# A second raw chunk in the startup of a hybrid decoder step: 256-column chunks for four column tiles, and what is rescaled later

## The chip, the cores and the metric

The kernel runs on one core of one Trainium2 chip. The metric is the device time of one execution in microseconds (us), as a median over runs. Engines are named as in the profile: PE (TensorE, matrix products; PEld its weight loads), DVE (VectorE), ACT (ScalarE), POOL (GpSimd), SP (SyncE, which issues most DMAs).

## The reference

One layer of a decoder trunk for 1024 prompt positions and 64 sample positions (8 sequences of 8), each a row of 1024 values. Cut to what matters:

```python
h = rmsnorm(x, g_norm)
proj = h @ w_in                       # 1024 x 3200, split into nine column groups
bg_a, cg_a, v_a, z_a, a_b, g_b, z_b, q_x, z_x = parts
conv_a = causal_dwconv(ctx_a, cg_a * v_a, w_conv_a, b_conv_a)       # 3 taps
out_a = bg_a * conv_a * silu(z_a)
u_b = a_b * sigmoid(g_b)
conv_b = causal_dwconv(ctx_b, u_b, w_conv_b, b_conv_b)              # 31 taps
out_b = silu(layernorm(conv_b)) * silu(z_b)
out_x = cross_attn(q_x, mk, mv) * silu(z_x)                         # 256 memory rows
y = rmsnorm(x + concat(out_a, out_b, out_x) @ w_out, g_final)
```

The new convolution states and the memory's keys and values are outputs too. All is float32.

## The kernel before, in words

**Products.** A float32 factor is split into a part `hi`, rounded to the form that PE takes at full rate, and the rest `lo`. Each product is three passes over the eight 128-row slabs of the 1024 channels: hi by hi, weights' lo by hi, weights' hi by activations' lo (`pass_`, `pass_k`). The transposed activations are `hh[k]` and `hl[k]` (k = 0 to 7), 1088 columns (positions) each; `w_in`'s columns are 25 tiles of 128 in the list `order`: a0, a1, a2, g0 (these four neighbour each other in `w_in` and share one load per slab, `hw_load`, `hw_hi`, `hw_lo`), then cg0, v0, bg0, g1, g2, q0, q1 and so on. A tile's positions are worked in chunks: the first `NHEAD` tiles use the list `HEAD`, all others `REST`. `proj(n, c)` is one tile and chunk: 24 products, then an eviction `evac` from PSUM.

**Normalising.** x is loaded as nine tiles of rows (`xt[0]` to `xt[8]`), transposed on PE (`x_tr`, four PSUM banks `SD` in turn), multiplied by g_norm and split (`x_ev_hi` on ACT, `x_ev_lo` on DVE). The row factor 1/rms is found by a `Norm` object: a square per row tile on ACT (`square`), a short chain (a root on ACT, five small DVE operations, `chain`, `factor`), and a scaling of each row tile (`scale` on DVE, `scale_act` on ACT). For chunk 0 the products start from raw, unscaled activations; the factor, as a row of 256 columns `rrow` on all partitions, is multiplied in when the bank is evicted (`take`, on DVE, where `rawc` is true; else a copy on ACT). Later `rescale(k)` brings `hh[k]` and `hl[k]` of that chunk to their scaled values for the tiles that come after: two DVE operations, an ACT copy, a DVE subtraction.

**Order.** `startup` is written out by hand, and its instructions keep the written order on each engine (`manual_schedule`). What comes after it is ordered by a planner with costs of its own, which may also place a ready later instruction between those of the startup. Side work is a list `steps`; `pass_` runs one of them after slab 3 and one after slab 7 (`None` is an empty place). Engines run their queues strictly in order. SBUF has 45 large buffers (`big`), PSUM four banks `MM` for products and four `SD` for the rest.

**The startup.** WARM products of the identity, the transposes of tiles 0 and 1, then the loop over slabs, in which `p(k, j)` is slab k, pass j, for four tiles of chunk 0; cg0's chunk 0 in a fifth bank (`pr4`); chunk 1 of all five with n1 (row tiles 2 to 4) scaled ahead; n2 (row tiles 5 to 8) scaled beside it; the transposes of chunk 2 as side steps of chunk 1's third pass. Then chunk 2 of the five tiles with the rescaling and the transposes of the parameters (`params_T`) as side work, and from tile 5 on three chunks per tile.

**Taps.** When g0's last chunk is evicted, `queue_taps` queues 31 operations of 1024 columns on DVE for each of three channel groups (the long convolution); `run_taps(taps_per(n))` issues some of them after each `proj`.

Of the kernel before, what the change touches and what calls it, by code (L numbers as in the profile page):

```python
# [12 lines left out]
ALU = mybir.AluOpType  # L13
# [14 lines left out]
L0, L1, L2 = 1, 3, 2  # L28
T1, T2 = 2, 2
TAPPRI = 100  # L30
WARM = 5

HEAD = [(0, 256), (256, 384), (640, 448)]
REST = [(0, 384), (384, 384), (768, 320)]
NHEAD = 5


NROW = 4
RAW = HEAD[0][1]


@with_exitstack
def hybrid_trunk_kernel(
# [62 lines left out]
    def dv(ns):  # L106
        dve_t[0] += ns
# [7 lines left out]
                taps.popleft()()  # L115

    def taps_per(n):
        return 3 if 5 <= n < 9 else T1 if n < 11 else T2

    def side():  # L120
        if steps:
# [42 lines left out]
    xt = [None] * 9  # L164
    xrows = [128] * 8 + [64]
    xcols = [i * 128 for i in range(9)]
    groups = [[0, 1], [2, 3, 4], [5, 6, 7, 8]]

    def x_src(i):
        return x_prompt[0, i * 128:(i + 1) * 128, :] if i < 8 else x_sample.rearrange("b t d -> (b t) d")  # L170
# [1 line left out]
    def x_load(i):  # L172
        xt[i] = xt[i] or B("x", cols=D)
        if xrows[i] < 128:
            G.memset(xt[i][xrows[i]:], 0.0)
        nc.sync.dma_start(xt[i][:xrows[i]], x_src(i))
# [42 lines left out]
    def rescale(k):  # L219
        a, b = hh[k][:, :RAW], hl[k][:, :RAW]  # L220
        t = B("t", cols=RAW)
        V.tensor_tensor(t, a.bitcast(F32), b.bitcast(F32), ALU.add)
        V.tensor_tensor(t, t, rrow[0], ALU.mult)
        S.copy(a, t)
        V.tensor_sub(b, t, a.bitcast(F32))
        dv(1000)

    def gm_T():
        ps = SD()
# [48 lines left out]
    def hw_load(k, q=nc.sync):  # L278
        if k % 2 == 0:
            hrw[k // 2] = B("wr", cols=D)  # L280
        c0 = order[0][2] * 128
        q.dma_start(hrw[k // 2][:, hsl(k)], w_in[0, k * 128:(k + 1) * 128, c0:c0 + 512])
# [9 lines left out]
        dv(602)  # L292

    def w_block(n, k, lo):
        if n < NROW:
            o = (k % 2) * 512 + n * 128
            return (hwl if lo else hwh)[k // 2][:, o:o + 128]
        return (wlo if lo else whi)[n][:, k * 128:(k + 1) * 128]
# [102 lines left out]

    rawc, rrow = [False], [None]

    def take(dst, ps, n):
        if rawc[0]:
            V.tensor_tensor(dst, ps[:, :n], rrow[0][:, :n], ALU.mult)
            dv(n / 0.96 + 70)
        else:
            S.copy(dst, ps[:, :n])
# [4 lines left out]
    def ev_a(c, ps, j):  # L414
        off, n, p, s = pieces(c)
        if c[0] == 0:
            u_p[j] = B("u")
            G.memset(u_p[j][:, 0:30], 0.0)
        take(u_p[j][:, 30 + off:30 + off + p], ps, p)
        if s:  # L420
            S.copy(us_new(j), tb(ps[:, p:n]))

    def ev_g(c, ps, j):
        off, n, p, s = pieces(c)
        if c[0] == 0:
            sig[j] = B("sig")
        if j == 0:
            take(sig[j][:, off:off + n], ps, n)
            if s:
                S.activation(sig[0], sig[0], AF.Sigmoid)  # L430
                V.tensor_tensor(u_p[0][:, 30:30 + SEQ], u_p[0][:, 30:30 + SEQ], sig[0][:, :SEQ], ALU.mult)
                dv(1140)
        else:
            S.activation(sig[j][:, off:off + n], ps[:, :n], AF.Sigmoid)  # L434
            u = u_p[j][:, 30 + off:30 + off + p]
            V.tensor_tensor(u, u, sig[j][:, off:off + p], ALU.mult)
            dv(p / 0.96 + 70)
        if s:
            V.tensor_tensor(us_new(j), us_new(j), tb(sig[j][:, SEQ:NT]), ALU.mult)
            V.tensor_copy(u_s[j][:, 304:334], u_p[j][:, SEQ:SEQ + 30])  # L440
            dv(250)
            queue_taps(j)
# [16 lines left out]
    def ev_cg(c, ps, j):  # L459
        off, n, _, _ = pieces(c)  # L460
        if c[0] == 0:
            cgt[0] = B("cg")
        take(cgt[0][:, off:off + n], ps, n)

    def ev_v(c, ps, j):
        off, n, p, s = pieces(c)
# [56 lines left out]
    def evac(n, c, ps):  # L523
        kind, j, _ = order[n]
        c = chunks(n)[c]
        rawc[0] = n < NHEAD and c[0] == 0
        if kind == "zA":
            ev_z(c, ps, j, tA[j])
        elif kind == "zB":
            ev_z(c, ps, 3 + j, accB[j])  # L530
        elif kind == "zX":
            ev_z(c, ps, 6 + j, aO[j])
        else:
            {"g": ev_g, "a": ev_a, "q": ev_q, "cg": ev_cg, "v": ev_v, "bg": ev_bg}[kind](c, ps, j)
# [461 lines left out]
    def startup():  # L996
# [8 lines left out]
        hw_load(2)  # L1005
        for i in (0, 1):
            x_half(i, 1, nc.sync)
        hw_load(3)
        x_load(2)
        hw_load(4)  # L1010
        hw_load(5)
        x_load(3)
        hw_load(6)
        hw_load(7)
        x_load(4)
        w_load(4)
        for i in range(5, 8):
            x_load(i)
        for k in range(KT):
            hh[k] = B("hh", F32R)  # L1020
# [4 lines left out]
        T.transpose(wps[:, 256:264], graw, ident[:8, :8])  # L1025
        V.tensor_copy(gT[:, 0:8], wps[:, 256:264])
        xt[8] = B("x", cols=D)
        norm = [Norm([xt[i] for i in g], [xrows[i] for i in g]) for g in groups]
        n0, n1, n2 = norm
        banks = [SD() for _ in range(4)]  # L1030

        def x0_tr(k, i):
# [2 lines left out]
        for i in (0, 1):  # L1035
            for k in range(4):
                x0_tr(k, i)
        acc = [MM() for _ in range(NROW)]

        def p(k, j):  # L1040
            for n in range(NROW):
                pass_k(n, 0, acc[n], j, k)

        def hi(k):
# [25 lines left out]
        mem_load()  # L1070
        load_params()
        nc.sync.dma_start(graw, g_mem[0].rearrange("(k p) -> k p", p=128))
        w_load(5)
        n0.square(0)
        hw_hi(3, S.copy)
        banks += [SD() for _ in range(4)]
# [7 lines left out]
        hw_lo(3)  # L1084
        for k in range(4, 8):
            lo(k)
        for k in range(3, KT):
            if k > 3:
                hw_hi(k, S.copy)
                hw_lo(k)  # L1090
            p(k, 0)
            p(k - 1, 1)
            p(k - 1, 2)
            if k == 5:
                n0.square(1)
                n0.chain()
                n0.factor()
                fb = B("fb", cols=RAW)
                for i in (0, 1):
                    V.tensor_scalar(  # L1100
                        fb[:, i * 128:i * 128 + 128], ident, 0.0, n0.f[:, i:i + 1], ALU.mult, ALU.add
                    )
            if k == 6:
                rps = SD()
                for i in (0, 1):
                    tr(rps[:, i * 128:i * 128 + 128], fb[:, i * 128:i * 128 + 128], 128)
                n1.square(0)
                rrow[0] = B("rrow", cols=RAW)
                S.copy(rrow[0], rps[:, :RAW])
        for n in range(NROW):  # L1110
            for j in (1, 2):
                pass_k(n, 0, acc[n], j, KT - 1)
        w_hi(4, G.tensor_copy)
        n1.square_v(1)
        n1.square(2)
        n1.chain()
        n1.factor()
        n1.scale_act(1)
        n1.scale(0)
        n1.scale(2)  # L1120
        w_lo(4)
        pr4 = SD()
        for n in range(NROW):
            evac(n, 0, acc[n])
        for j, (lo_, h) in enumerate(((False, hh), (False, hl), (True, hh))):
            for k in range(KT):
                mm(
                    pr4[:, :RAW], w_block(4, k, lo_), h[k][:, :RAW],
                    j == 0 and k == 0, j == 2 and k == KT - 1, RAW / 2.4,
                )  # L1130
        evac(4, 0, pr4)
        t1 = [x_tr(1, k) for k in range(3)]
        pr = [MM() for _ in range(NROW)]
        for k in range(KT):
            x_ev(1, k, t1[k])
            for n in range(NROW):
                pass_k(n, 1, pr[n], 0, k)
            if k + 3 < KT:
                t1.append(x_tr(1, k + 3))
        for i in range(4):  # L1140
            n2.square(i)
        n2.chain()
        n2.scale(0)
        n2.scale(1, G)
        n2.scale(2)
        n2.scale(3)
        for n in range(NROW):
            pass_(n, 1, pr[n], 1)
        mem_norm()
        for k in range(KT):  # L1150
            steps.append(mk(x_T, 2, k))
        for n in range(NROW):
            pass_(n, 1, pr[n], 2)
            evac(n, 1, pr[n])
        pr4 = MM()
        for j in range(3):
            pass_(4, 1, pr4, j)
        evac(4, 1, pr4)
        flush_steps()


    if True:
        with tc.manual_schedule():
            startup()
        for n in range(0, NCT):
            if n < NHEAD:
                if n == 0:
                    for k in range(KT):
                        steps += [mk(rescale, k)]
                    for h in range(2):  # L1170
                        steps.append(mk(w_split, NHEAD, h))
                    for j in range(3):
                        steps += [mk(params_T, j), None]
                    steps.append(gm_T)
                if n == 2:
                    w_load(NHEAD + 1)
            else:
                w_load(n + 2)
            kind, j, _ = order[n]
            if n == NHEAD:  # L1180
                for q in range(2):
# [68 lines left out]
            if n == 23:  # L1250
                for k in (0, 1):
                    steps += [None, mk(wo_split, worder[k], 0), None, mk(wo_split, worder[k], 1)]
                wo_load(worder[2])
            for c in range(3) if n >= NHEAD else (2,):
                proj(n, c)
                if c < 2:
                    w_split(n + 1, c)
# [57 lines left out]
```

## Time and profile before

| | |
|---|---|
| median of 3 runs | 478.25 us (477.37 to 479.23) |
| profiled execution, its own time | 477.41 us |
| its span | 475.3 us, 7295 instructions |
| busy: PE, DVE, ACT, POOL | 462.9, 325.5, 223.6, 8.2 us |
| chain that ended last | PE 67%, DVE 23%, ACT 5%, issue 3%, DMA 2% of the span |
| moved by DMA | 40.42 MB, mean 85 GB/s |

A row of a timeline gives the start, the duration (of a group: from its first start to its last end; products overlap, so the distance to the next group's start says what a group costs), the engine, the line, what was written from what, and in brackets how long the engine had been idle before and what released it. A row of waits gives the total, the count and the longest. Times are from the span's start.

### The profile page before, as it was taken

The numbers are of one execution on the slowest core, as the hardware profiler recorded it, in microseconds if no ns is written. First come the engines' busy times: TensorE is split into PE (matmuls) and PEld (weight loads), VectorE is DVE, ScalarE is ACT, GpSimd is POOL, SyncE is SP. The second block draws the span as 40 slices with busy tenths as digits, with TensorE's granted clock in tenths as the row PEclk, the third lists the DMA queues.
The fourth block names the chain that finished last, engine by engine and source line by source line (L and its number), as shares of the span: only waits on it lengthen the run. The fifth ranks groups of instructions, "written<-read, shape, count | busy, mean of one in ns | idle before, by whom it ended". The sixth has DMA issues, their size and how long they took to land.

```text
span 475.3 us, 7295 instructions
## 1 busy us (share of the span) xinstructions
PE 462.9 (97%) x2827; PEld 431.1 (91%) x2827; DVE 325.5 (68%) x576; ACT 223.6 (47%) x581; POOL 8.2 (2%) x24
## 2 busy tenths in 40 slices
PE   8999999999999999999999999999999999999994
PEld 7889989999999998999999999899999988888884
DVE  3768824999999999998589498733563547333334
ACT  5657513803427338546692464657863524211111
POOL 3101000000000000000000000000000000000000
PEclk9999999999999999999999999999999999999998
DMA  8940412210027300111020531022401643311111
GB/s 297 361 137 0 137 41 90 88 46 1 1 83 217 101 0 1 44 46 46 0 71 20 171 96 38 9 60 90 150 28 45 187 190 112 133 46 44 44 62 71
DMA packets 36446, 40.42 MB, mean 85 GB/s; under 512 B 1743, under 2 KB 30325, under 8 KB 36405
## 3 DMA queue, kind: packets, MB, share of 16 engines
q1 hardware_dynamic: 36109, 39.44, 25.8%
q10 hardware_dynamic: 304, 0.53, 0.4%
q8 instruction: 22, 0.36, 0.3%
q14 instruction: 11, 0.09, 0.1%
HBM read 34.81 MB, written 5.42 MB: 85 GB/s over the span
## 4 chain that ended last, share of the span: by engine, by line
PE 67%; DVE 23%; ACT 5%; issue 3%; DMA 2%; ACTq 0%; DVEq 0%; SPq 0%
PE mm L96 58%; DVE accB L60 11%; PE sd L103 5%; PE sd L96 3%; DVE wl L60 2%; DVE tA L60 2%; DVE Q L60 1%; DVE red L60 1%; DVE mx L60 1%; ACT sd L882 1%; DVE x L60 1%; ACT junk L188 1%; DMA wr<-in_w_in_dram 1%; DVE wml L60 1%; DMA graw<-in_g_norm_dram 1%
## 5 line engine op out<-in xcount | busy, mean ns | idle before, releaser
L96 PE MATMUL mm<-hh,wh 128*128 128x384 f32 (+3 forms) x592 | 117.1, 334 | 1.6 <-ACT wh L288 1.0
L96 PE MATMUL mm<-hl,wh 128*128 128x384 f32 (+3 forms) x592 | 116.8, 332 | 0.0
L60 DVE SCALAR_TENSOR_TENSOR accB<-u,prm,accB 128x1024 f32<-128x1024 f32 x90 | 115.2, 1281 | 1.2
L96 PE MATMUL mm<-hh,wl 128*128 128x384 f32 (+3 forms) x592 | 113.9, 330 | 0.0
L96 PEld LDWEIGHTS mm<-hh,wh 128*128 128x128 f32 x592 | 99.1, 190 | 5.2 <-ACT wh L288 1.5
L96 PEld LDWEIGHTS mm<-hl,wh 128*128 128x128 f32 x592 | 98.3, 188 | 2.0 <-issue 1.3
L96 PEld LDWEIGHTS mm<-hh,wl 128*128 128x128 f32 x592 | 99.0, 188 | 1.3 <-issue 0.3
L96 PE MATMUL mm<-woh,ml 128*128 128x512 f32 (+1 forms) x136 | 51.2, 377 | 0.0
L96 PE MATMUL mm<-wol,mh 128*128 128x512 f32 (+1 forms) x136 | 51.2, 377 | 0.0
L96 PE MATMUL mm<-woh,mh 128*128 128x512 f32 (+1 forms) x136 | 51.2, 377 | 0.0
L60 DVE TENSOR_TENSOR xres<-mm,xres 128x512 f32<-128x512 f32 (+2 forms) x19 | 12.4, 662 | 39.4 <-PE mm L96 39.2
L60 DVE TENSOR_TENSOR wl<-wr,wh 128x512 fp32r<-128x512 f32 x50 | 33.3, 686 | 5.1 <-ACT wh L288 2.7
L945 ACT ACTIVATE sd<-xres 128x512 f32<-128x512 f32 (+1 forms) x16 | 9.6, 600 | 57.6 <-DVE xres L60 57.6
L96 PEld LDWEIGHTS mm<-woh,mh 128*128 128x128 f32 x136 | 25.6, 188 | 4.7
L96 PEld LDWEIGHTS mm<-wol,mh 128*128 128x128 f32 x136 | 25.6, 188 | 4.7
L96 PEld LDWEIGHTS mm<-woh,ml 128*128 128x128 f32 x136 | 25.6, 188 | 4.6
L363 ACT ACTIVATE prod<-us,prm 128x64 f32<-128x64 f32 x93 | 24.0, 343 | 0.9 <-DVE wl L60 0.8
L713 ACT ACTIVATE P<-sd,nb 128x256 f32<-128x256 f32 x32 | 14.8, 474 | 18.9 <-DVE nb L60 18.8
L311 ACT CAST wh<-wr 128x512 fp32r<-128x512 f32 x40 | 23.3, 625 | 0.0
L511 ACT ACTIVATE sz<-mm 128x384 f32<-128x384 f32 (+1 forms) x24 | 11.3, 472 | 20.2 <-PE mm L96 20.2
L250 ACT ACTIVATE hh<-sd,gT 128x256 fp32r<-128x256 f32 (+2 forms) x24 | 12.8, 564 | 10.7 <-PE sd L103 10.4
L434 ACT ACTIVATE sig<-mm 128x384 f32<-128x384 f32 (+1 forms) x6 | 2.8, 473 | 31.4 <-PE mm L96 31.4
(206 smaller groups left out, 526.2 us busy)
## 6 DMA issues: line engine op xcount, KB each, us to landing
wr<-in_w_in_dram SPq DMA_DIRECT2D x21, 512.0 KB
wor<-in_w_out_dram SPq DMA_DIRECT2D x8, 512.0 KB
xres<-in_x_prompt_dram SPq DMA_DIRECT2D x8, 512.0 KB
out_dram<-xres SPq DMA_DIRECT2D x7, 512.0 KB
x<-in_x_prompt_dram SPq DMA_DIRECT2D x6, 512.0 KB
cache<-in_cache_mem_k_dram SPq DMA_DIRECT2D x8, 256.0 KB
cache<-in_cache_mem_v_dram SPq DMA_DIRECT2D x8, 256.0 KB
wr<-in_w_in_dram SPq DMA_DIRECT2D x7, 256.0 KB
```

Source lines behind the costliest of these rows:

```text
L60: r = f(*a, **k)
L96: T.matmul(out, lhsT, rhs, start=start, stop=stop)
L103: T.transpose(out, in_, ident[:n, :n])
L188: S.activation(junk[:r], self.ts[i][:r], AF.Square, accum_out=self.ss[:r, i:i + 1])
L250: S.activation(hh[k][:, off:off + n], ps[:, :n], AF.Copy, scale=gT[:, k:k + 1])
L311: S.copy(dst_hi[:, a:b], src[:, a:b])
L363: S.activation(p3[:, k, :], src, AF.Copy, scale=w[:, k0 + k:k0 + k + 1])
L434: S.activation(sig[j][:, off:off + n], ps[:, :n], AF.Sigmoid)
L511: S.activation(sz[0][:, off:off + n], ps[:, :n], AF.Silu)
L713: S.activation(P_[i][:, h * 256:h * 256 + 256], bank[h // 2][:, (h % 2) * 256:(h % 2) * 256 + 256], AF.Exp, bias=nb[:, h:h + 1], scale=SCA ...
L882: S.activation(junk[:, :384], t, AF.Square, bias=lst["nmu"][:, i:i + 1], accum_out=lst["sq"][:, i:i + 1])
L945: S.activation(junk[:rows], xr[:rows, cs], AF.Square, accum_out=ss[:rows, f:f + 1])
```

## The change

Four tiles instead of five are worked in `HEAD` chunks, and there are four such chunks of 256, 256, 256 and 320 columns instead of three of 256, 384 and 448. Chunks 0 and 1 of these tiles both start from raw activations (RAW = 512); `rrow` holds two scale rows of 256 and, beside each, the diagonal that is transposed into it (`r_bc`, `r_tr`, `r_cp`). `rescale` works on 512 columns. n1 is now row tiles 2 and 3 (only a factor, no scaling), n2 tiles 4 and 5, n3 tiles 6 to 8. cg0 becomes an ordinary tile with `REST` chunks; its weights are loaded behind the parameters. The hi and lo parts of slab 7 come ahead of the copy of the first scale row. x tile 2 is loaded behind slab 5 and tile 3 behind slab 7. There are nine warm-up products instead of five. In the last chunk the order of the tiles is a0, g0, a1, a2, and the taps per `proj` are 3 below tile 4, then 2. The memory's norm moves from the startup to a side step.

```diff
-WARM = 5
-HEAD = [(0, 256), (256, 384), (640, 448)]
+WARM = 9
+HEAD = [(0, 256), (256, 256), (512, 256), (768, 320)]
-NHEAD = 5
-NROW = 4
-RAW = HEAD[0][1]
+NHEAD = 4
+RAW = 512
-        return 3 if 5 <= n < 9 else T1 if n < 11 else T2
+        return 3 if n < NHEAD else T1 if n < 11 else T2
-    groups = [[0, 1], [2, 3, 4], [5, 6, 7, 8]]
+    groups = [[0, 1], [2, 3], [4, 5], [6, 7, 8]]
...
-        V.tensor_tensor(t, t, rrow[0], ALU.mult)
+        V.tensor_tensor(t, t, rrow[0][:, RAW:], ALU.mult)
...
-        rawc[0] = n < NHEAD and c[0] == 0
+        rawc[0] = n < NHEAD and c[0] < RAW
...
+        def r_bc(norm, off):
+            norm.chain()
+            norm.factor()
+            for i in (0, 1):
+                o = off + i * 128
+                V.tensor_scalar(rrow[0][:, o:o + 128], ident, 0.0, norm.f[:, i:i + 1], ALU.mult, ALU.add)
+        def r_tr(off):
+            ps = SD()
+            for i in (0, 1):
+                o = off + i * 128
+                tr(ps[:, i * 128:i * 128 + 128], rrow[0][:, o:o + 128], 128)
+            return ps
+        def r_cp(off, ps):
+            S.copy(rrow[0][:, RAW + off:RAW + off + 256], ps[:, :256])
...
             if k == 6:
-                rps = SD()
-                for i in (0, 1):
-                    tr(rps[:, i * 128:i * 128 + 128], fb[:, i * 128:i * 128 + 128], 128)
-                n1.square(0)
-                rrow[0] = B("rrow", cols=RAW)
-                S.copy(rrow[0], rps[:, :RAW])
+                rps = r_tr(0)
+                t1 += [x_tr(1, 0), x_tr(1, 1)]
+        r_cp(0, rps)
+        x_ev_hi(1, 0, t1[0])
+        x_ev_hi(1, 1, t1[1])
+        for n in range(NHEAD):
             for j in (1, 2):
                 pass_k(n, 0, acc[n], j, KT - 1)
-        (cg0's weight split, n1's squares, chain and three scalings, cg0's 24 products of chunk 0)
             evac(n, 0, acc[n])
+        t1 += [x_tr(1, 2), x_tr(1, 3)]
+        acc = [MM() for _ in range(NHEAD)]
         for k in range(KT):
+            if k > 1:
+                x_ev_hi(1, k, t1[k])
+            x_ev_lo(1, k, t1[k])
+            for n in range(NHEAD):
+                pass_k(n, 1, acc[n], 0, k)
+            if k + 4 < KT:
+                t1.append(x_tr(1, k + 4))
+        n1.square(0)
+        n1.square(1)
+        r_bc(n1, 256)
+        n2.square(0)
+        n2.square(1)
+        n2.chain()
+        n2.factor()
+        n2.scale_act(0)
+        n2.scale(1)
+        for n in range(NHEAD):
+            pass_(n, 1, acc[n], 1)
+        rps = r_tr(256)
+        r_cp(256, rps)
+        steps.extend([None, None])
         for k in range(KT):
             steps.append(mk(x_T, 2, k))
+        for i in range(3):
+            n3.square(i)
+        for n in range(NHEAD):
+            pass_(n, 1, acc[n], 2)
+            evac(n, 1, acc[n])
         flush_steps()
+        n3.chain()
+        n3.scale(0)
+        n3.scale(1)
+        n3.scale(2)
...
+        for k in range(KT):
+            steps.append(mk(x_T, 3, k))
+        for k in range(KT):
+            steps += [mk(rescale, k), None]
+        for n in range(NHEAD):
+            proj(n, 2)
+        w_load(NHEAD + 1)
+        for h in range(2):
+            steps.append(mk(w_split, NHEAD, h))
+        steps.append(mem_norm)
+        for j in range(3):
+            steps += [mk(params_T, j), None]
+        steps.append(gm_T)
+        for n in (0, 3, 1, 2):
+            proj(n, 3)
+        flush_steps()
```

More of the change, by code (lines that the diff above doesn't have):

```diff
@@ L222, in rescale @@
         V.tensor_tensor(t, a.bitcast(F32), b.bitcast(F32), ALU.add)
-        V.tensor_tensor(t, t, rrow[0], ALU.mult)
+        V.tensor_tensor(t, t, rrow[0][:, RAW:], ALU.mult)
         S.copy(a, t)
         V.tensor_sub(b, t, a.bitcast(F32))
-        dv(1000)
+        dv(1900)
     def gm_T():
@@ L294, in w_block @@
     def w_block(n, k, lo):
-        if n < NROW:
+        if n < NHEAD:
             o = (k % 2) * 512 + n * 128
@@ L402, in hybrid_trunk_kernel, with take @@
     rawc, rrow = [False], [None]
-    def take(dst, ps, n):
+    def take(dst, ps, off, n):
         if rawc[0]:
-            V.tensor_tensor(dst, ps[:, :n], rrow[0][:, :n], ALU.mult)
+            V.tensor_tensor(dst, ps[:, :n], rrow[0][:, RAW + off:RAW + off + n], ALU.mult)
             dv(n / 0.96 + 70)
@@ L418, in ev_a @@
             G.memset(u_p[j][:, 0:30], 0.0)
-        take(u_p[j][:, 30 + off:30 + off + p], ps, p)
+        take(u_p[j][:, 30 + off:30 + off + p], ps, off, p)
         if s:
@@ L427, in ev_g @@
         if j == 0:
-            take(sig[j][:, off:off + n], ps, n)
+            take(sig[j][:, off:off + n], ps, off, n)
             if s:
@@ L462, in ev_cg @@
             cgt[0] = B("cg")
-        take(cgt[0][:, off:off + n], ps, n)
+        take(cgt[0][:, off:off + n], ps, off, n)
     def ev_v(c, ps, j):
@@ L1007, in startup @@
             x_half(i, 1, nc.sync)
-        hw_load(3)
+        for k in (3, 4, 5):
+            hw_load(k)
         x_load(2)
[L1010 to L1017, printed above, removed]
+        for k in (6, 7):
+            hw_load(k)
+        for i in range(3, 8):
             x_load(i)
@@ L1027, in startup @@
         xt[8] = B("x", cols=D)
-        norm = [Norm([xt[i] for i in g], [xrows[i] for i in g]) for g in groups]
-        n0, n1, n2 = norm
+        n0, n1, n2, n3 = (Norm([xt[i] for i in g], [xrows[i] for i in g]) for g in groups)
+        rrow[0] = B("rrow", cols=2 * RAW)
+        def r_bc(norm, off):
[4 more added lines that the diff above has]
+                V.tensor_scalar(rrow[0][:, o:o + 128], ident, 0.0, norm.f[:, i:i + 1], ALU.mult, ALU.add)
+            dv(500)
+        def r_tr(off):
[6 more added lines that the diff above has]
+            S.copy(rrow[0][:, RAW + off:RAW + off + 256], ps[:, :256])
         banks = [SD() for _ in range(4)]
@@ L1037, in startup @@
                 x0_tr(k, i)
-        acc = [MM() for _ in range(NROW)]
+        acc = [MM() for _ in range(NHEAD)]
         def p(k, j):
-            for n in range(NROW):
+            for n in range(NHEAD):
                 pass_k(n, 0, acc[n], j, k)
@@ L1072, in startup @@
         nc.sync.dma_start(graw, g_mem[0].rearrange("(k p) -> k p", p=128))
-        w_load(5)
+        w_load(NHEAD)
         n0.square(0)
@@ L1086, in startup @@
             lo(k)
+        t1 = []
         for k in range(3, KT):
@@ L1095, in startup @@
                 n0.square(1)
-                n0.chain()
-                n0.factor()
-                fb = B("fb", cols=RAW)
-                for i in (0, 1):
-                    V.tensor_scalar(
-                        fb[:, i * 128:i * 128 + 128], ident, 0.0, n0.f[:, i:i + 1], ALU.mult, ALU.add
-                    )
-            if k == 6:
-                rps = SD()
-                for i in (0, 1):
-                    tr(rps[:, i * 128:i * 128 + 128], fb[:, i * 128:i * 128 + 128], 128)
-                n1.square(0)
-                rrow[0] = B("rrow", cols=RAW)
-                S.copy(rrow[0], rps[:, :RAW])
@@ L1110, in startup @@
-        for n in range(NROW):
+                r_bc(n0, 0)
+            if k == 6:
+                rps = r_tr(0)
[4 more added lines that the diff above has]
+        for n in range(NHEAD):
             for j in (1, 2):
                 pass_k(n, 0, acc[n], j, KT - 1)
[L1113 to L1123, printed above, removed]
-            evac(n, 0, acc[n])
[L1125 to L1132, printed above, removed]
@@ L1133, in startup @@
-        pr = [MM() for _ in range(NROW)]
-        for k in range(KT):
[L1135 to L1141, printed above, removed]
-        n2.chain()
[L1143 to L1149, printed above, removed]
+            evac(n, 0, acc[n])
@@ new lines, in startup @@
+        t1 += [x_tr(1, 2), x_tr(1, 3)]
+        acc = [MM() for _ in range(NHEAD)]
+        for k in range(KT):
+            if k > 1:
[10 more added lines that the diff above has]
+        n2.square(1)
+        n2.chain()
+        n2.factor()
@@ L1150, in startup @@
+        n2.scale_act(0)
[5 more added lines that the diff above has]
+        steps.extend([None, None])
         for k in range(KT):
             steps.append(mk(x_T, 2, k))
[L1152 to L1158, printed above, removed]
+        for i in range(3):
+            n3.square(i)
@@ L1164, in hybrid_trunk_kernel @@
             startup()
[L1165 to L1178, printed above, removed]
+        for k in range(KT):
+            steps.append(mk(x_T, 3, k))
+        for k in range(KT):
+            steps += [mk(rescale, k), None]
+        for n in range(NHEAD):
+            proj(n, 2)
[9 more added lines that the diff above has]
+        flush_steps()
+        for n in range(NHEAD, NCT):
+            w_load(n + 2)
             kind, j, _ = order[n]
@@ L1253, in hybrid_trunk_kernel @@
                 wo_load(worder[2])
-            for c in range(3) if n >= NHEAD else (2,):
+            for c in range(3):
                 proj(n, c)
```

## The prediction

> **What bounds the kernel now.** I read first the page's shares by engine, then the waits of TensorE, then the windows by stage, then the timelines of the first 60 us, where all of the change lies. The share and the waits:
>
> ```profile
> PE 462.9 (97%) x2827; PEld 431.1 (91%) x2827; DVE 325.5 (68%) x576; ACT 223.6 (47%) x581; POOL 8.2 (2%) x24
> ```
>
> ```profile
> PE mm L1024 <- POOL ss L183: 1.4, 1, 1.4
> PE sd L96 <- ACT PT L733: 1.1, 2, 0.6
> PE mm L96 <- ACT wh L288: 1.0, 1, 1.0
> PE mm L1025 <- DMA graw<-in_g_norm_dram: 0.8, 1, 0.8
> PE sd L96 <- DVE wl L60: 0.7, 1, 0.7
> PE mm L96 <- ACT wh L311: 0.6, 1, 0.6
> ACT L713 <- DVE nb L60: 8.3, 1, 8.3
> ```
>
> TensorE is busy in 462.9 of 475.3 us, so there are 12.4 us to win at most, and whatever adds products adds time. The list says where the idle time is: 1.0 + 0.7 us in the startup (1.0 for the hi part of the eighth weight slab, 0.7 for the lo part of cg0's weights), and 1.1 + 0.6 us at the start of attention, where ScalarE had itself waited 8.3 us for VectorE.
>
> ```profile
> 57.00:79.00 22.00, 22.00 (x114) 19.95 (x113) 3.98 (x15) 4.71 (x9) 0.10 (x1) 1.00 0.27 82
> 83.00:226.00 143.00, 141.30 (x901) 136.64 (x900) 140.05 (x186) 70.70 (x212) 0.10 (x1) 1.00 0.20 56
> ```
>
> After the core's window and its length the columns are the busy time of TensorE, of its weight loads, of VectorE and of ScalarE. VectorE has 18.0 us free just before the taps begin, and none (140.05 of 143) while they run.
>
> **The start.** The page's clock column reads 1.00 here, but the durations show a slow array up to about 8.6 us:
>
> ```profile
> 1.39 2.50 PE L1024 MATMUL mm<-ident 128*128 128x128 f32 x10 [1.39 <-POOL ss L183]
> 4.94 1.97 PE L103 MATMUL sd<-ident,x 128*128 128x128 f32 x8
> 6.93 2.17 PE L96 MATMUL mm<-hh,wh 128*128 128x256 f32 x8
> 8.93 0.64 PE L96 MATMUL mm<-hh,wl 128*128 128x256 f32 x4
> 9.41 0.64 PE L96 MATMUL mm<-hl,wh 128*128 128x256 f32 x4
> 10.37 1.04 PE L103 MATMUL sd<-ident,x 128*128 128x128 f32 x8
> 11.16 0.72 PE L96 MATMUL mm<-hh,wl 128*128 128x256 f32 x4
> ```
>
> ```profile
> 6.31 0.84 ACT L250 ACTIVATE hh<-sd,gT 128x256 fp32r<-128x256 f32 x2 [2.64 <-PE sd L103]
> 7.45 0.62 ACT L288 CAST wh<-wr 128x512 fp32r<-128x512 f32 x1 [0.30 <-DMA wr<-in_w_in_dram]
> 18.38 0.37 ACT L1109 COPY rrow<-sd 128x256 f32<-128x256 f32 x1 [1.73 <-PE sd L103]
> 18.65 0.62 ACT L288 CAST wh<-wr 128x512 fp32r<-128x512 f32 x1
> 17.75 1.17 POOL L319 CAST wh<-wr 128x512 fp32r<-128x512 f32 x2 [8.28 <-DMA wr<-in_w_in_dram]
> ```
>
> Eight transposes take 1.99 us at first (to the next group's start) and 0.79 us later. Ten warm-up instructions take 2.50 us, so the eighteen of nine products, without a gap, end near 5.7 us: past 4.94, where the transposes now start. If the array is fast from there on, the fifth transpose, which frees the first ScalarE eviction, ends near 6.55 us instead of 6.3 us; the second slab's cast still waits for its DMA at 7.45, so the second group of products stays at 8.1 us, and the four groups from there to p(2,0), the third slab's first products, then take 0.48 us each: end near 10.03 us, 0.34 us earlier than the 10.37 us of before. If the array becomes fast at 8.6 us as before, the fifth transpose ends near 7.1 us, the chain to p(2,0) runs through ScalarE (four evictions of 0.42, two casts of 0.62: 10.05 us), and its group ends near 10.55 us: 0.18 us later. I take -0.1 us, ends -0.34 and +0.18. The Trainium skill ("TensorE: Matmul & The Clock Gate", Part 1: The HAM clock gate) has the array's clock opened by a free-running busy window of about 3.4 us; by it the unbroken warm-up would open it somewhere from 4.8 to 8.2 us, which gives the same sum within 0.1 us; the opening seen here, at 8.6 us after an array without a gap since 4.73, agrees with such a window.
>
> **The stall before the eighth slab goes (-0.98).** ScalarE's queue held the cast of slab 7 (18.65) behind the copy of the scale row (18.38), which waited for two transposes on TensorE. The copy now comes after the loop, so the cast follows slab 6's and is bounded by its data alone. Those came before 17.75 less two 512 KB loads; now one 512 KB load fewer precedes them. Ends: -0.98 and, if the data were only just there, -0.7.
>
> **The removed waits (-1.5).** cg0 leaves the startup, and with it its weights' lo wait (0.75). In the chunk boundaries of before there is 0.25 us ahead of chunk 1, and 0.5 us here: four transposes in 0.89 us, where 10.37 to 11.16 gives 0.4:
>
> ```profile
> 40.58 1.14 PE L103 MATMUL sd<-ident,x 128*128 128x128 f32 x4
> 41.47 0.94 PE L96 MATMUL mm<-hl,wh 128*128 128x384 f32 x4
> ```
>
> **TensorE's own work (+0.8).** Start to start of whole groups:
>
> ```profile
> 50.99 1.55 PE L96 MATMUL mm<-hh,wl 128*128 128x384 f32 x8
> 52.37 1.55 PE L96 MATMUL mm<-hl,wh 128*128 128x384 f32 x8
> 55.41 1.81 PE L96 MATMUL mm<-hh,wl 128*128 128x448 f32 x8
> 57.06 1.81 PE L96 MATMUL mm<-hl,wh 128*128 128x448 f32 x8
> 89.75 1.33 PE L96 MATMUL mm<-hh,wh 128*128 128x320 f32 x8
> 90.91 1.33 PE L96 MATMUL mm<-hh,wl 128*128 128x320 f32 x8
> ```
>
> 256 columns take 0.12 us, 320: 0.145, 384: 0.1725, 448: 0.206. A column tile has 24 products per chunk: before 24x(0.12+0.1725+0.206) = 11.96, now 24x(3x0.12+0.145) = 12.12, so +0.16 for each of four tiles; cg0 goes to 24x(2x0.1725+0.145) = 11.76, -0.2. Two more transposes for the second scale row: +0.2. With 0.2 for the shorter groups' hand-overs: +0.8 (ends +0.4, +1.0).
>
> **A new wait at chunk 2 (+2.5).** This is the disputed term. The startup's order is kept as written, and ScalarE now has in its queue, one behind another: last eviction of chunk 1, two squares (n1), root, two squares (n2), root, one scaling, the row's copy, three squares (n3), and only then the evictions of chunk 2, which free the four banks that TensorE transposes into.
>
> ```profile
> 32.91 1.05 ACT L188 ACTIVATE junk<-x 128x1024 f32<-128x1024 f32 x1
> 33.95 1.05 ACT L188 ACTIVATE junk<-x 128x1024 f32<-128x1024 f32 x1
> 21.23 0.30 ACT L147 ACTIVATE y<-ss,epst 128x3 f32<-128x3 f32 x1 [0.92 <-DVE ss L60]
> 22.57 1.15 ACT L206 ACTIVATE x<-x,f 128x1024 f32<-128x1024 f32 x1 [1.04 <-DVE f L60]
> ```
>
> ```profile
> L60 DVE SCALAR_TENSOR_TENSOR hl<-sd,gT,hh 128x256 fp32r<-128x256 f32 x8 | 3.4, 478 | 1.6 <-ACT hh L250 1.6
> ```
>
> A square costs 1.04 us from start to start, root to scaling 1.34, the scaling 1.15, an eviction 0.42 on ScalarE and 3.4/8 = 0.43 on VectorE. Let S be the start of chunk 1's products. ScalarE: last transposes of chunk 1 at S+3.0 (four groups of 0.48, four pairs at 0.2, 0.3 for VectorE to free the first bank), eviction 3.45, squares 5.55, root 5.85, squares 7.95, scaling from 9.3 to 10.45, copy 10.8, squares 13.9, first eviction of chunk 2 14.3, its lo part on VectorE 14.75. TensorE: first pass S+4.95, second 8.8, scale row 9.0, then 28 products and four pairs of transposes: 13.15, where the fifth pair needs that bank. It waits 1.6 us. Two more pairs then wait for VectorE, which has two row-scaled evictions (0.42 each) between: 0.4. With the 0.3 and 0.2 for hand-overs: +2.5. What would cover it is other TensorE work that the planner may draw in (parameter and memory transposes, about 2.5 us): low end +0.4. High end: the rival below. The last group's scaling (three at 0.8 on VectorE) ends near S+22; the planner places what needs it, and chunk 2 runs 13 us, so it costs nothing.
>
> **Rescaling and taps (-0.6).**
>
> ```profile
> L60 DVE TENSOR_TENSOR wl<-wr,wh 128x512 fp32r<-128x512 f32 x50 | 33.3, 686 | 5.1 <-ACT wh L288 2.7
> L60 DVE TENSOR_TENSOR t<-hh,hl 128x256 f32<-128x256 f32 x8 | 3.1, 405 | 0.0
> ```
>
> Rescaling has 24 operations; at 512 columns (686 ns) instead of 256 (405): +6.7 us of VectorE; the row-scaled evictions +1.3. They lie beside chunks 2 and 3, where VectorE had 18.0 us free; without that cover cg0 would start up to 8 us late. The gate tile second lets the taps begin two tiles earlier: 9 taps in chunk 3, and 42 to the end of q instead of 48 in fewer tiles. VectorE should then be less behind at attention, where ScalarE waited 8.3 us for it and TensorE 1.7 us for ScalarE. Ends 0 and -1.7; I take a third. Loads change order only; cg0's weights are due at about 66 us, long after the parameters that now precede them.
>
> **Sum.** 477.41 (span 475.3 and 2.1 around it) -0.1 -0.98 -1.5 +0.8 +2.5 -0.6 = 477.5. That execution is 0.84 us under the median of 478.25; I do not know whether its luck comes again and add half: 478.0, no change (this kernel's runs can tell 0.5%, 2.4 us).
>
> **The rivals.** *Side work in the chains* (slower). The planner may slip ready operations between the startup's:
>
> ```profile
> 41.32 0.15 DVE L60 RECIPROCAL y<-y 128x2 f32<-128x2 f32 x1
> 41.39 0.40 DVE L60 TENSOR_TENSOR t<-hh,hl 128x256 f32<-128x256 f32 x1
> 41.72 0.14 DVE L60 TENSOR_TENSOR t<-y,v 128x2 f32<-128x2 f32 x1
> ```
>
> Here rescaling sits inside the memory norm's chain. Now one such add is 0.69 us, and cg0's absence leaves buffers for more. Three to six in the chains of n1 and n2 put the scaling, and with it the three squares and chunk 2, back by 2.0 to 4.1 us: 480.0 to 482.1, middle 481.1; four to five decide (2.6 us). Against it: n2's chain had none before. *Cover and calm* (faster): the planner fills the wait (-2.0) and attention's waits go wholly (-1.1): 474.9. For it: those transposes wait for nothing but loads; against it: it must foresee the wait. *A late gate*: if the long warm-up does not open the clock and the four groups up to p(2,0) run slowly (0.85 instead of 0.48 each), +0.2 + 4x0.37 = 1.7: 479.7. The Trainium skill (same page, Part 4: PE-mode transpose) says that transposes do not count as busy for the gate, which would bring this about. Against it: the array was fast at 8.9 us after 2 us of transposes in the 3.4 us before.
>
> **How the numbers follow.** Forecast 0.50; side work 0.22, nearly all over 480.6; cover and calm 0.20; late gate 0.08. The forecast's own ends, with its small terms, are 476.3 to 480. The range takes in both larger rivals up to a tail each: 475.2 to 481.8. Faster by over 0.5% (under 475.9) 0.21, slower (over 480.6) 0.23, between 0.56.
>
> **What would show it.** Right: no TensorE wait on the eighth slab's cast; one of 1 to 2 us on a transpose of chunk 2, released by VectorE's lo eviction behind three squares on ScalarE; 320-column groups where 448 stood; VectorE busy in 45 to 65 us; attention's waits at or under 1.7. Wrong: rescaling adds inside the n1 or n2 chain; transposes of the parameters inside the wait; a wait for cg0's rescaled columns near 65 us, which I price at nothing; first products later than 7.5 us.

## The result, and the profile after

The changed kernel takes 475.42 us (475.39 to 475.79 over 4 runs) where before took 478.15 us (477.37 to 479.23): a ratio of 0.9947, interval 0.9933 to 0.9961. That is 0.53% faster by the ratio and 0.57% by the two medians, and 2.6 us under the forecast of 478.0 us: just inside the range of 475.2 to 481.8, just past the bound of 0.5% that the forecast stayed within, and in the part that had a chance of 0.21. The profiled execution took 475.39 us with a span of 473.4 us, 1.9 us shorter than before.

The page's shares, the list of TensorE's waits, and the windows (the columns after the window's length are TensorE, its weight loads, VectorE, ScalarE). Of the windows the first line is of the kernel before, the other three are of the kernel after:

```profile
PE 463.8 (98%) x2933; PEld 435.2 (92%) x2933; DVE 332.7 (70%) x592; ACT 228.4 (48%) x596; POOL 4.8 (1%) x21
```

```profile
PE mm L1019 <- POOL ss L182: 1.4, 1, 1.4
PE mm L95 <- ACT hh L249: 1.1, 2, 0.8
PE mm L95 <- ACT wh L287: 0.4, 1, 0.4
PE sd L102 <- DVE lnx L59: 0.2, 1, 0.2
PE sd L102 <- ACT x L205: 0.2, 1, 0.2
```

```profile
120.00:160.00 40.00, 40.00 (x237) 38.88 (x236) 39.69 (x51) 17.76 (x52) 0.00 (x0) 1.00 0.37 106
```

```profile
57.00:79.00 22.00, 22.00 (x147) 21.64 (x146) 21.77 (x48) 15.12 (x35) 0.10 (x1) 1.00 0.42 124
120.00:160.00 40.00, 40.00 (x242) 39.41 (x241) 34.94 (x49) 12.12 (x28) 0.00 (x0) 1.00 0.42 119
160.00:200.00 40.00, 40.00 (x277) 39.12 (x276) 37.63 (x51) 26.70 (x88) 0.10 (x1) 1.00 0.09 27
```

TensorE is busy 0.9 us longer, with 1.7 us more of warm-up in it (4.21 against 2.50), and idle 2.8 us less. The waits for cg0's weights, for slab 7 and for the memory's norm weights (`graw`) are gone, and so are both of attention's. Three have come: 0.33 us on ScalarE's evictions at 7.14 us and 0.36 us on one of its casts at 8.21 us, both in the start, and 0.76 us on the evictions at 36.17 us. VectorE's free time moved: 18.0 us before the taps became 0.2, and in exchange it is no longer full from 120 us on (34.94 of 40, where before had 39.69).

Where the time went is read from two fixed points: the start of the last chunk of q0 (tile 9), and that of the last chunk of the projection's last tile. Between them both kernels do the same products (1501 and 1502 recorded). First before, then after:

```profile
149.19 0.31 PE L96 MATMUL mm<-hh,wh 128*128 128x320 f32 x1
370.55 0.45 PE L96 MATMUL mm<-hh,wh 128*128 128x320 f32 x2
```

```profile
149.56 0.31 PE L95 MATMUL mm<-hh,wh 128*128 128x320 f32 x1
368.74 0.31 PE L95 MATMUL mm<-hh,wh 128*128 128x320 f32 x1
```

At q0 the changed kernel is 0.37 us *late*. All that it gains, 2.18 us, it gains between there and the end of the projection, in a part of the program whose code did not change: TensorE's idle time in it falls from 1.86 to 0.15 us, and its busy time by 0.47 us for the same products. The rebuilt startup paid nothing in this execution; the experiments below say whether the taps' new timing paid for all.

The startup after, TensorE first:

```profile
1.38 4.21 PE L1019 MATMUL mm<-ident 128*128 128x128 f32 x18 [1.38 <-POOL ss L182]
5.72 1.09 PE L102 MATMUL sd<-ident,x 128*128 128x128 f32 x8
8.21 0.74 PE L95 MATMUL mm<-hh,wh 128*128 128x256 f32 x4 [0.36 <-ACT wh L287]
10.23 1.03 PE L102 MATMUL sd<-ident,x 128*128 128x128 f32 x8
34.70 0.71 PE L95 MATMUL mm<-hl,wh 128*128 128x256 f32 x4
36.17 1.11 PE L95 MATMUL mm<-hh,wh 128*128 128x256 f32 x3 [0.76 <-ACT hh L249]
37.11 0.38 PE L102 MATMUL sd<-ident,x 128*128 128x128 f32 x2
```

and ScalarE's queue ahead of the wait:

```profile
31.22 1.15 ACT L205 ACTIVATE x<-x,f 128x1024 f32<-128x1024 f32 x1 [1.02 <-DVE f L59]
32.53 1.06 ACT L187 ACTIVATE junk<-x 128x1024 f32<-128x1024 f32 x1
34.62 1.04 ACT L187 ACTIVATE junk<-x 64x1024 f32<-64x1024 f32 x1
35.66 1.53 ACT L249 ACTIVATE hh<-sd,gT 128x256 fp32r<-128x256 f32 x4
```

The eight transposes from 5.72 us take 1.09 us where before took 1.97. After the four products of 34.70 us TensorE has nothing ready until the evictions, which begin at 35.66, directly behind the last of n3's three squares. The planner then put the first products of chunk 2 (36.17) ahead of the fifth pair of transposes (37.11), so the list puts the wait down to the eviction itself.

### The profile page after: what moved, and what is told of

It reads as the page before. It is cut to its first block, busy times and chain, and to the rows that moved or that the text cites. A ratio compares the mean times of both kernels' runs of the same rounds, so it can differ in the third digit from the quotient of the medians.

```text
span 473.4 us, 7529 instructions
## 1 busy us (share of the span) xinstructions
PE 463.8 (98%) x2933; PEld 435.2 (92%) x2933; DVE 332.7 (70%) x592; ACT 228.4 (48%) x596; POOL 4.8 (1%) x21
## 3 DMA queue, kind: packets, MB, share of 16 engines
q1 hardware_dynamic: 36109, 39.44, 26.2%
## 4 chain that ended last, share of the span: by engine, by line
PE 93%; ACT 3%; DMA 1%; DVE 1%; issue 0%; ACTq 0%; DVEq 0%
PE mm L95 81%; PE sd L95 7%; PE sd L102 5%; DMA wr<-in_w_in_dram 1%; ACT sd L881 1%; ACT junk L187 1%; PE sd L866 1%; ACT L146 0%; ACT wh L310 0%; DVE t L59 0%; ACT mh L512 0%; ACT sz L510 0%; ACT wh L287 0%; ACT lnx L868 0%; ACTq L1001 0%
## 5 line engine op out<-in xcount | busy, mean ns | idle before, releaser
L95 PE MATMUL mm<-hh,wh 128*128 128x384 f32 (+2 forms) x632 | 120.1, 325 | 1.4 <-ACT hh L249 1.1
L95 PE MATMUL mm<-hl,wh 128*128 128x384 f32 (+2 forms) x632 | 118.3, 323 | 0.0
L95 PE MATMUL mm<-hh,wl 128*128 128x384 f32 (+2 forms) x632 | 116.5, 322 | 0.0
L95 PEld LDWEIGHTS mm<-hh,wh 128*128 128x128 f32 x632 | 102.1, 188 | 4.6 <-ACT hh L249 1.7
L95 PEld LDWEIGHTS mm<-hl,wh 128*128 128x128 f32 x632 | 101.5, 189 | 1.5 <-issue 1.3
L95 PEld LDWEIGHTS mm<-hh,wl 128*128 128x128 f32 x632 | 101.6, 188 | 0.7 <-issue 0.3
L310 ACT CAST wh<-wr 128x512 fp32r<-128x512 f32 x42 | 24.7, 625 | 0.0
L249 ACT ACTIVATE hh<-sd,gT 128x256 fp32r<-128x256 f32 (+1 forms) x32 | 14.0, 490 | 8.8 <-PE sd L102 8.7
```

What stands on the lines that cost most here:

```text
L95: T.matmul(out, lhsT, rhs, start=start, stop=stop)
L249: S.activation(hh[k][:, off:off + n], ps[:, :n], AF.Copy, scale=gT[:, k:k + 1])
L310: S.copy(dst_hi[:, a:b], src[:, a:b])
```

## The experiments

Theories at the outset. *Taps*: attention's waits went because VectorE has fewer taps waiting when attention begins. Its rival: they went because the memory's keys and values are worked one tile earlier. *Squares*: the new wait is ScalarE's queue order. *Clock*: part of the difference of the medians is the slow start of TensorE's array.

**Nine and five warm-up products.** The changed kernel with five:

```diff
-WARM = 9
+WARM = 5
```

> The changed kernel with five warm-up products instead of nine, nothing else. Theory (the long warm-up opens the array's clock in the startup at a steady early time): the slow array returns up to 8.6 us or later, by an amount that differs from run to run; the end of the third slab's first products moves from 10.23 us to 10.4 us or more, the median rises by 0.3 to 1.2 us (475.7 to 476.6), and the spread over the runs grows from 0.4 us to over 1 us. Rival (the start is bound by the loads, the clock does not matter): median within 0.2 us of 475.4 and a spread as small as with nine.

Measured: 476.01 us (475.64 to 476.70, 5 runs), ratio to before 0.9963 (0.9951 to 0.9976). Its timeline shows the slow array past 9 us:

```profile
9.32 1.05 PE L95 MATMUL mm<-hh,wl 128*128 128x256 f32 x4
10.17 0.68 PE L95 MATMUL mm<-hl,wh 128*128 128x256 f32 x4
```

A group costs 0.85 us at 9.32 and 0.52 at 10.17. The median is 0.6 us above that of the changed kernel, but the intervals of the two ratios overlap. The kernel before with nine:

```diff
-WARM = 5
+WARM = 9
```

> The kernel before with nine warm-up products instead of five, nothing else. Theory (clock): the spread of 1.9 us over the runs of before falls under 0.6 us and the median falls by 0.6 to 1.0 us, to about 477.3. Rival (the spread has another cause): same spread and median as before, 478.2 give or take 0.3.

Measured: 477.16 us (477.02 to 477.64, 11 runs) where 27 runs of before gave 477.68 (476.74 to 479.49); ratio 0.9988 (0.9978 to 0.9997). Nine products cut the spread, the highest time less the lowest, from 2.75 to 0.62 us (standard deviation 0.59 and 0.19) and the median by 0.5 us, 0.1 to 1.0 by the interval, a little under the 0.6 to 1.0 that I expected.

The kept traces show why. The distance from one product to the next, 0.21 us at first and later 0.11 to 0.12, says when the array becomes fast: between 4.3 and 5.7 us in the seven kernels with nine warm-up products, between 8.2 and 10.2 us in the four with five. The third slab's first products end between 10.17 and 10.40 us in the seven and between 10.25 and 11.17 in the four. The clock theory holds, as one cause of the spread and not the only one: the kernel with more taps below has nine products and spreads over 1.74 us in 11 runs, the kernel before with the new taps has five and spreads over 1.06.

**The taps.** The gate tile last again in the changed kernel:

```diff
-        for n in (0, 3, 1, 2):
+        for n in (0, 1, 2, 3):
```

> The changed kernel with the last chunk's tiles in the order a0, a1, a2, g0, so that the taps begin two tiles (some 7 us) later and 3 instead of 9 are issued in that chunk; nothing else. Theory (the waits of attention went because VectorE's taps are further ahead there): some of the waits return, TensorE idle 0.4 to 1.7 us between 165 and 210 us, time 475.8 to 477.1. Rival (they went because the memory's keys and values are worked one tile earlier): no wait returns, 475.4 give or take 0.2.

Measured: 478.17 us (477.90 to 478.55, 11 runs), ratio 1.0006 (0.9996 to 1.0016): the whole gain of the change is gone, more than I had priced. Two of the new waits are where I had not looked, at the sample attention (near 277 and 306 us), the third is at attention (178 us):

```profile
PE sd L102 <- DVE Ps L59: 0.8, 1, 0.8
PE sd L95 <- DVE Pts L59: 0.7, 1, 0.7
PE mm L95 <- ACT wh L310: 0.6, 1, 0.6
```

The reverse, the kernel before with the gate tile second and the changed tap rule:

```diff
-        return 3 if 5 <= n < 9 else T1 if n < 11 else T2
+        return 3 if n < 4 else T1 if n < 11 else T2
...
-        for n in range(0, NCT):
+        for n in [0, 3, 1, 2] + list(range(4, NCT)):
```

> The kernel before with the gate tile second in its last head chunk (order a0, g0, a1, a2, cg0) and the tap rule of the changed kernel (3 per tile and chunk below tile 4, then 2 to tile 10, then 2); nothing else. Theory (taps): the waits of attention (1.7 us in the list of waits) go, 1.7 to 2.2 us less than before: 476.0 to 476.5. Rival (the memory's keys and values, or the second raw chunk): the waits stay, 478.2 give or take 0.4.

Measured: 476.67 us (476.20 to 477.26, 11 runs), ratio 0.9978 (0.9969 to 0.9987), just above the expected 476.0 to 476.5. The waits at attention went, with the memory's order as before, so the rival falls; but a wait like those of the last run came at 304 us and took 0.7 us back, which the theory as put did not say:

```profile
PE sd L103 <- DVE Ps L60: 0.7, 1, 0.7
```

More taps per tile, in the changed kernel:

```diff
-        return 3 if n < NHEAD else T1 if n < 11 else T2
+        return 3 if n < NHEAD or 5 <= n < 9 else T1 if n < 11 else T2
```

> The changed kernel with 3 instead of 2 taps per tile and chunk for tiles 5 to 8, as in the kernel before: 63 instead of 51 taps issued to the end of q; nothing else. Theory (what TensorE waits for at attention is the backlog of issued taps on VectorE: 13 issued and not done at 166 us before, 7 now): the backlog grows past that of before and waits of 1 to 4 us come at attention or ahead of it, 476.4 to 479.4. Rival (an early start of the taps is enough, whatever the rate): 475.4 give or take 0.3.

Measured: 477.56 us (477.08 to 478.82, 11 runs), ratio 0.9994 (0.9983 to 1.0004). The wait is back at attention, at the same 1.7 us as before, with VectorE full from 120 to 160 us (39.55 of 40):

```profile
PE sd L95 <- ACT PT L732: 1.7, 1, 1.7
```

The run with the gate last had changed two things, when the taps start and how many are issued by the end of q1. The last run of this row keeps the late start and restores the number:

```diff
-        return 3 if n < NHEAD else T1 if n < 11 else T2
+        return 3 if n < NHEAD or n in (5, 6) else T1 if n < 11 else T2
...
-        for n in (0, 3, 1, 2):
+        for n in (0, 1, 2, 3):
```

> The changed kernel with the order a0, a1, a2, g0 in the last chunk, as in the run with the gate tile last, but with 3 instead of 2 taps per chunk for tiles 5 and 6, so that 51 taps are issued to the end of q, as in the changed kernel, and 45 were in that run; nothing else. Theory (what counts is how many taps are left for the time after q): the waits at the sample attention (0.8 and 0.7 us) go, time 475.4 to 476.3. Rival (what counts is the early start): waits stay, 477.4 to 478.4.

Measured: 475.28 us (475.12 to 475.71, 5 runs), ratio 0.9949 (0.9936 to 0.9962): all of the gain, without the early start. No wait of TensorE stands after 45 us but one of 0.2. VectorE is as full from 120 to 160 us as with more taps (39.40 of 40), so its busy share doesn't decide.

Between the two fixed points the kernels take 221.36 us (before), 219.18 (after), 221.81 (gate last), 220.26 (before with the new taps) and 219.17 (gate last with the number restored). Changing the taps alone takes away all that the changed kernel gains there, and more, and gives the kernel before half of it: the taps' new timing paid for the gain between the two points.

The groups of taps between 57 and 166 us, as VectorE did them: before, after, gate last, six more (with the gate second), and gate last with the number restored.

```profile
L60 DVE SCALAR_TENSOR_TENSOR accB<-u,prm,accB 128x1024 f32<-128x1024 f32 x37 | 47.2, 1281 | 0.5
```

```profile
L59 DVE SCALAR_TENSOR_TENSOR accB<-u,prm,accB 128x1024 f32<-128x1024 f32 x42 | 53.7, 1280 | 0.7
```

```profile
L59 DVE SCALAR_TENSOR_TENSOR accB<-u,prm,accB 128x1024 f32<-128x1024 f32 x38 | 48.7, 1281 | 0.7
```

```profile
L59 DVE SCALAR_TENSOR_TENSOR accB<-u,prm,accB 128x1024 f32<-128x1024 f32 x46 | 58.9, 1280 | 0.6
```

```profile
L59 DVE SCALAR_TENSOR_TENSOR accB<-u,prm,accB 128x1024 f32<-128x1024 f32 x42 | 53.8, 1280 | 0.6
```

With the two first taps of a group (another operation) these are 39, 44, 40, 48 and 44 done. Set beside what the code had queued by then (the queue's entries to the end of q1, without those that are not taps: 48, 47, 42, 58, 47; the expectation of the run with more taps had counted those in, and so said 13 and 7 where the table has 9 and 3), and beside when the last tap ran:

| kernel | taps queued by the end of q1 | done at 166 us | pending | last tap, us | TensorE waits at attention | at the sample attention |
|---|---|---|---|---|---|---|
| before | 48 | 39 | 9 | 301.7 | 1.7 | 0 |
| more taps | 58 | 48 | 10 | 289.0 | 1.7 | 0 |
| after | 47 | 44 | 3 | 301.2 | 0 | 0 |
| gate last, same number | 47 | 44 | 3 | 301.2 | 0 | 0 |
| before, new taps | 43 | 41 | 2 | 308.4 | 0 | 0.7 |
| gate last | 42 | 40 | 2 | 312.4 | 0.6 | 1.5 |

So there are two sides. Nine or ten taps pending when attention starts stand ahead of its small operations on VectorE and cost 1.7 us. The small operation is `nb`, the negated maximum that ScalarE's exponential needs. Before, then after:

```profile
172.55 1.28 DVE L60 SCALAR_TENSOR_TENSOR accB<-u,prm,accB 128x1024 f32<-128x1024 f32 x1
173.74 0.16 DVE L60 TENSOR_SCALAR nb<-mx 128x4 f32<-128x4 f32 x1
173.98 1.28 ACT L713 ACT_TABLE_LOAD   x1 [8.26 <-DVE nb L60]
178.15 0.97 PE L96 MATMUL mm<-hh,wh 128*128 128x384 f32 x4 [0.61 <-ACT wh L311]
```

```profile
171.97 0.16 DVE L59 TENSOR_SCALAR nb<-mx 128x4 f32<-128x4 f32 x1
172.24 1.28 ACT L712 ACT_TABLE_LOAD   x1 [6.14 <-DVE nb L59]
```

`nb` comes 1.77 us earlier after, although q0's last chunk starts 0.37 us later. ScalarE's cast of the next tile's weights, queued behind the exponentials, comes as much earlier (175.70 instead of 177.45 us), and TensorE no longer waits for it.

On the other side, too few taps done by then leave taps running past 305 us, where one stands ahead of `Ps`, the sample attention's normalised weights (0.8 us with the gate last, 0.7 in the kernel before with the new taps, where a tap at 303.23 is followed by `Ps` at 304.43). The changed kernel sits between. When its taps are done matters less: with the gate last and the number restored VectorE keeps 5.3 us free at 57 to 79 us, and four more taps fall behind 120 us instead.

Two waits of the last row come from elsewhere. The 0.7 us near 277 us goes back to another entry of the same queue: the sum of the samples' products (1.99 us at 267.43) stands ahead of the sample attention's maximum (269.33). The 0.6 us at 178 us is the planner's order on ScalarE: the casts of weights (177.79) stand behind four scalings of P (175.94), where the changed kernel has them ahead (175.70).

**The three squares.** The changed kernel with n3's squares behind chunk 2's transposes:

```diff
         for k in range(KT):
             steps.append(mk(x_T, 2, k))
-        for i in range(3):
-            n3.square(i)
         for n in range(NHEAD):
             pass_(n, 1, acc[n], 2)
             evac(n, 1, acc[n])
         flush_steps()
+        for i in range(3):
+            n3.square(i)
         n3.chain()
```

> The changed kernel with the three squares of n3 after the transposes of chunk 2 instead of before them in ScalarE's queue; nothing else. Theory (the squares hold the evictions that TensorE waits for at 35 us): the waits of TensorE on ScalarE's evictions there (1.1 us in the list of waits, 1.5 us with the hand-overs) go and no other comes, 473.8 to 474.4. Rival A (the wait only moves: n3's factor comes 2 to 3 us later and the transposes of chunk 3 wait for it): 475.2 to 476. Rival B (the wait is for the scaling of tiles 4 and 5, not for the squares): 475.4 give or take 0.2.

Measured: 473.99 us (473.74 to 474.82, 6 runs), ratio to before 0.9922 (0.9909 to 0.9935). The place that waited:

```profile
35.45 0.72 PE L95 MATMUL mm<-hl,wh 128*128 128x256 f32 x4
36.01 0.82 PE L102 MATMUL sd<-ident,x 128*128 128x128 f32 x6
36.59 1.49 PE L95 MATMUL mm<-hh,wh 128*128 128x256 f32 x8
```

TensorE runs through. The first 320-column group starts at 51.21 us where it was 52.70: the wait was worth 1.5 us (1.4 by the medians), it was the squares, and nothing took its place. This version beats both kernels.

**Rescaling, more of it.** The version with the late squares, with one operation of each rescaling done twice:

```diff
         V.tensor_tensor(t, a.bitcast(F32), b.bitcast(F32), ALU.add)
+        V.tensor_tensor(t, a.bitcast(F32), b.bitcast(F32), ALU.add)
```

> The kernel of the late squares with the first operation of every rescaling done twice: eight more VectorE operations of 512 columns, 0.69 us each, 5.5 us in all; nothing else. Theory (rescaling is hidden beside chunks 2 and 3, and the taps catch up before attention): no change, 474.0 give or take 0.3. Rival A (VectorE, full from 57 to 120 us, passes it on: cg0 waits near 64 us for its rescaled columns): 1 to 4 us more. Rival B (it reaches attention as backlog): waits of 0.5 to 2 us between 165 and 310 us.

Measured: 473.77 us (473.64 to 474.22, 4 runs), ratio 0.9917 (0.9904 to 0.9930). Sixteen of these additions instead of eight:

```profile
L59 DVE TENSOR_TENSOR t<-hh,hl 128x512 f32<-128x512 f32 x16 | 10.4, 684 | 0.0
```

5.5 us more of VectorE work cost nothing: rescaling's part on VectorE is covered, and its price at 512 columns (0.69 us an operation) is what I had taken. The additions run between 38 and 63 us, and VectorE's busy time up to 120 us hardly changes: the taps move back, into 120 to 160 us, where it is now busy 39.44 of 40 us instead of 35.92.

**The queue order at slab 7 alone.** One line of the kernel before moved:

```diff
                 n1.square(0)
                 rrow[0] = B("rrow", cols=RAW)
-                S.copy(rrow[0], rps[:, :RAW])
+        S.copy(rrow[0], rps[:, :RAW])
```

> The kernel before with one line moved: the copy of the scale row on ScalarE comes after the loop over slabs, so that the cast of slab 7 is queued ahead of it. Theory (the stall of 0.98 us before slab 7 is ScalarE's queue order): TensorE's wait for that cast goes and the tiles after it come 0.8 to 1.0 us earlier, the time falls by as much, to 476.7 to 476.9 where before is 477.7. Rival A (given back: cg0's lo part is ready no earlier, its wait grows from 0.75 to 1.7 us): same time as before within 0.3. Rival B (slab 7's data are late anyway): the wait stays.

Measured: 476.41 us (475.72 to 477.83, 10 runs), ratio 0.9971 (0.9959 to 0.9983), 1.4 us less, between 0.8 and 2.0 by the interval:

```profile
17.84 0.38 PE L103 MATMUL sd<-ident,fb 128*128 128x128 f32 x2
17.98 0.72 PE L96 MATMUL mm<-hh,wh 128*128 128x256 f32 x4
```

```profile
PE sd L96 <- DVE wl L60: 0.6, 1, 0.6
```

Slab 7 follows the transposes at once (it had stood at 19.32, behind 0.98 us of idle time), and the wait for cg0's weights did not grow. Rivals A and B fall. The loads of x are those of before here, so the order alone removes the wait.

## Why the prediction was right or wrong

**As a whole.** The forecast's own ends, 476.3 to 480, do not hold the measured 475.42 us. The stated range does, because it was widened for the rival *cover and calm*; that it holds is in part luck.

**The start: right in the profiled execution, wrong in the median.** -0.14 us was measured (10.37 to 10.23), -0.1 was said. The -0.1 lay between two cases, and the first came, with an array that is fast from about 5.7 us on; it had been put at 10.03, and came 0.2 us later because the second group started at 8.21 instead of 8.1 and cost 0.58 instead of 0.48. So the fit of the number is partly luck. Then I added half of the 0.84 us by which the profiled execution lay under the median, not knowing its cause. A cause is the array's slow start, which ends at 8.2 to 10.2 us with five warm-up products and at 4.3 to 5.7 with nine: the median of after lies 0.03 us from its profiled execution. I had the mechanism and its bounds in hand, and drew from it no change in the spread: 0.4 us of the miss. The two profiled executions differ by 2.0 us and the ratio gives 2.5; the 0.5 between is what nine products gained in the kernel before.

**Slab 7: right.** The wait is gone, and the line alone is worth 0.8 to 2.0 us, with 0.98 said. **cg0's wait: right**, it is gone. The terms for chunk boundaries and for TensorE's own work (+0.8) were not measured by themselves.

**The new wait at chunk 2: the mechanism right, the size too large.** ScalarE's order and times came out as written: with S = 21.23 us, the start of chunk 1's products, the first eviction of chunk 2 started at S+14.4, where I had 13.9. Undoing it gave 1.5 us against the 1.6 + 0.4 that I charged for it, and the planner put three of chunk 2's own products (0.36 us) into it, a filler I had not named (I had thought of parameters and memory). All startup terms together, without taps and clock, stood at +0.7 with the start's -0.1 in; the fixed point at q0 says +0.37.

**Rescaling at nothing: right** for its part on VectorE, by the doubled operation. **The taps: the term that failed.** I wrote -0.6, a third of 1.7, with an end of -1.7. Measured between the fixed points: -2.18. The mechanism was the one named (less pending on VectorE at attention), and I had counted the taps, 42 against 48 after the head; but I took a third without asking how many would be *pending*. VectorE's 18 us of free time less the 8 us of added work hold, as an estimate, some 8 taps of 1.28 us; the trace shows five gained (44 done against 39) and one fewer queued. A count like that would have said that the queue is nearly empty at attention and the waits go wholly. Beyond the 1.7 us of listed waits TensorE's busy time for the same products fell by 0.47 us, so the end of -1.7 was too near; what that 0.47 consists of was not looked at.

**The rivals.** *Side work in the chains* did not come: the chains of n1 and n2 were untouched. The planner did draw rescaling into the startup, in a gap of VectorE, and into the chain of n3:

```profile
33.00 1.28 DVE L59 TENSOR_TENSOR t<-hh,hl 128x512 f32<-128x512 f32 x2
41.15 0.15 DVE L59 TENSOR_TENSOR t<-y,v 128x3 f32<-128x3 f32 x1
41.22 0.69 DVE L59 TENSOR_TENSOR t<-t,rrow 128x512 f32<-128x512 f32 x1
41.82 0.16 DVE L59 TENSOR_TENSOR t<-t,y 128x3 f32<-128x3 f32 x1
```

There it cost TensorE nothing: no wait stands between 39 us and the end of chunk 3. *Cover and calm* came half, the calm whole and the cover in part; it had been given 0.20. *A late gate* did not come with nine products, and is what the changed kernel with five shows (groups of 0.85 us still at 9.3 us). I cited for it the rule that transposes do not count for the clock gate (the Trainium skill, "TensorE: Matmul & The Clock Gate", Part 4: PE-mode transpose); no run here decides it, since with nine products the array was fast before the second transpose. For the moment at which the array becomes fast I had worked out 4.8 to 8.2 us from the free-running window of about 3.4 us that the Trainium skill gives (the same page, Part 1: The HAM clock gate). The traces agree only in part: five of the seven became fast at 5.2 to 5.7 us, two at 4.3, which is 2.9 us after the first product at 1.38.

## What to carry to other kernels

When side work is moved, count the operations queued and not done on the engine at the next place where something short must pass, not only the engine's busy share: 9 or 10 pending taps cost 1.7 us here, 3 cost nothing, and too few done earlier cost 0.7 to 0.8 us later. In a startup whose order is fixed by hand, write each engine's queue down and look for the long operations ahead of an eviction that another engine waits for: two moves of one to three instructions gave 1.4 us each by the medians, over half of what the whole change gave (2.5 us by the ratio). And before adding a term for luck, ask which mechanism makes the runs differ, and whether the change touches it.

## What the runs showed of the hardware that I had not expected

When the array becomes fast varies by enough to show in the spread of a 478 us kernel: at 8.2 to 10.2 us in four traces with five warm-up products, at 4.3 to 5.7 us in seven with nine, and the spread was 2.75 us over 27 runs against 0.62 over 11 of the same kernel. And 5.5 us of additional VectorE work left the time as it was (473.77 against 473.99 us) although VectorE was already busy 16.0 of the 17 us from 40 to 57 us and 21.6 of the 22 us after that: an engine that looks full still had slack, because the taps behind it were due later and found 3.5 us of free time at 120 to 160 us.
